# A two-layer decoder trunk on one core: operations recorded and ordered by a list scheduler inside the kernel, fixed tile homes, and another head

## The chip, the core and the metric

The kernel runs on one core of a Trainium2 chip. Such a core has a matrix engine (TensorE, PE in the profile; its weight loads are the row PEld), three engines for elementwise work (VectorE or DVE, ScalarE or ACT, GpSimd or POOL), and SyncE (SP), whose queue issues nearly all DMAs here. Every engine runs its own list of instructions strictly in the order in which the program holds it, and waits on semaphores for the others. The metric is the device time of one execution in microseconds, the median over runs.

## The reference, cut to what matters

Everything is float32, one batch, 256 positions, width 1024, two layers.

```python
def even_layer(x, ...):                       # layer 0
    h = rms_norm(x, norm_g)
    (nq, nkc, nvc, nks, nvs, nkw, nvw, ng, nz, mq, mk, mv, mz, eq, ez) = split(h @ w_in)
    kc, vc = nsa_compress(rot(nkc)), nsa_compress(nvc)          # blocks of 32 positions, small MLP
    a_out = nsa_attention(rot(nq), kc, vc, rot(nks), nvs, rot(nkw), nvw, sigmoid(ng + gate_b))
    b_out = moba_attention(rot(mq), rot(mk), mv)                # 8 heads, causal within 256
    m_out = memory_attention(eq, rms_norm(mem), w_mem_kv)       # 4 heads, 256 memory rows
    return x + concat(a_out*silu(nz), b_out*silu(mz), m_out*silu(ez)) @ w_out

def odd_layer(x, ...):                        # layer 1
    h = rms_norm(x, norm_g)
    rq, rk, rv, rz, eq, ez = split(h @ w_in)                    # 4 heads, 256 wide keys, 512 wide values
    r_out = head_group_norm(retention(rot(rq), rot(rk), rv))
    m_out = memory_attention(eq, mem_n, w_mem_kv)
    return x + concat(r_out*silu(rz), m_out*silu(ez)) @ w_out

def reference(x, mem, ...):
    return rms_norm(odd_layer(even_layer(x)), final_norm_g)
```

## The kernel before, in words

**Products.** A product with a weight matrix is made in units of eight rows of 128 input features, 512 output columns each. A weight chunk of 128x1024 floats (512 KB) is loaded from HBM into one of six `raw` buffers (`load`, L87). `split` (L118) makes two halves of it that the fast matmul format can hold: ACT casts it to `whi` (L122), DVE subtracts to get `wlo` (L123). `mm3` (L133) then multiplies three times: high by high, high by low, low by high. A chunk so costs one DMA, one ACT pass, one DVE pass and 12 matmuls of 512 columns on PE, or 24 of 256 columns in the products that come out transposed (`turned_unit`, L152).

**Order of the program.** First the head: the gate columns `nz` are multiplied while x itself arrives (L280 to L339), with three matmuls on a zeroed tile ahead of it (L320) so that PE has something to do. Then the layer-0 projections (`sparse_keys` with the weights `ksw`, `sparse_queries` with `nq`, `compress`, and so on), the four `sparse_pair`s, `memory_group`, the four `block_pairs`, the output projection, the same again for layer 1, and the final norm. Attention works on pairs of heads: scores into the two PSUM banks `s` (half-array matmuls, L100), a masked maximum on DVE (L451), an exponential on ACT (L453), scaling (L463, L465), three 128x128 transposes on PE into the single bank `t` (L252), a copy out of it by ACT (`pt`, L466), and then the products with the values into the single bank `o` (L100, again half-array). The bank `t` serves one of the two heads of a pair at a time: the second head's transposes wait for ACT's copy of the first.

**What sets the order.** The tile framework's own scheduler orders the instructions of each engine from a timeline of its own; only the first DMAs on SP and ACT are fixed by hand (L301). Tiles come from pools with a number of buffers for each tag (`raw` 6, `v4` 8, `s2` 8, `whi` and `wlo` 4); PSUM banks are `pj` 3, `s` 2, and `tr`, `t`, `o` one each. PE fills the waits of an attention chain with matmuls of a projection that comes later in the program.

Of the kernel before, what the change touches and what calls it, by code (L numbers as in the profile page):

```python
# [21 lines left out]
NV = 8  # L22
NS = 8
# [27 lines left out]

@with_exitstack
def trunk(
# [22 lines left out]
    V, S, G, PE = nc.vector, nc.scalar, nc.gpsimd, nc.tensor  # L76
    count = [0]

    def tl(tag, shape, bufs=1, dt=F32):
        count[0] += 1  # L80
        return sb.tile(shape, dt, tag=tag, bufs=bufs, name=f"{tag}_{count[0]}")

    def bank(tag):
        count[0] += 1
        return pp.tile([P, 512], F32, tag=tag, bufs=BANKS[tag], name=f"{tag}_{count[0]}")

    def load(t, src):  # L87
        nc.sync.dma_start(t, src)
        return t

    def after(ins, *others):

        for other in others:
            tc.add_manual_dep(ins.ins, other.ins.name,
                              mybir.DependencyInfo(mybir.DependencyClass.Sync, mybir.DependencyReason.DATA), reason="pair")

    def side_by_side(todo, *others):

        for i, (out, lhs, rhs, start, stop, *shared) in enumerate(todo):
            ins = PE.matmul(out, lhs, rhs, start=start, stop=stop, skip_group_check=bool(shared))  # L100
            if i == 0:
                after(ins, *others)
            else:
                tc.keep_in_program_order(ins)
# [13 lines left out]
    def split(raw, cols, tag=None):  # L118

        hi = tl(tag or "whi", [P, 1024], NV if tag else 4, F32R)[:, :cols]  # L120
        lo = tl(tag or "wlo", [P, 1024], NV if tag else 4, F32R)[:, :cols]
        S.copy(hi, raw)  # L122
        V.tensor_tensor(lo, raw, hi.bitcast(F32), ALU.subtract)  # L123
        return hi, lo
# [124 lines left out]
    def transposes(blocks, tag="t"):  # L249
        b = bank(tag)  # L250
        for i, a in enumerate(blocks):
            PE.transpose(b[:, i * P : (i + 1) * P], a, ident)  # L252
        return b[:, : P * len(blocks)]
# [27 lines left out]
    warm = tl("p", [P, 2, 512], 3)[:, 0]  # L281
    V.memset(warm, 0.0)
# [3 lines left out]
    xrow = [tl("v4", [P, D], NV) for _ in range(2)]  # L286
# [9 lines left out]
    xraw, wraw = [], []  # L296
    for q in range(4):
        if q % 2 == 0:
            xraw.append(tl("raw", [P, 1024], NRAW).rearrange("p (k t) -> p k t", k=4))
        wraw.append(tl("raw", [P, 1024], NRAW))  # L300
    with tc.manual_schedule(engines={mybir.EngineType.SP, mybir.EngineType.Activation}):  # L301
        nc.scalar.dma_start(gain0, vec[:, V_G0 : V_G0 + KT])
# [6 lines left out]
        for q in range(1, 4):
            load(xraw[q // 2][:, 2 * (q % 2) : 2 * (q % 2) + 2], xT[:, 2 * q : 2 * q + 2])  # L310
            load(wraw[q], w512[q // 2][:, (q % 2) * 1024 : (q % 2 + 1) * 1024])
        load(vect, vec)
        load(cpak, cst)
        load(posi, pos)
        load(posr, posrow.to_broadcast([P, T]))
        ahead = [load(tl("raw", [P, 1024], NRAW), w512[2][:, u * 1024 : (u + 1) * 1024]) for u in range(2)]
        for tok in range(2):
            load(xrow[tok], xtok[:, tok])
    wb = bank("t")
    for _ in range(3):  # L320
        PE.matmul(wb[:, :256], warm[:, 0:P], warm[:, :256], start=True, stop=True)
# [8 lines left out]
    for kt in range(KT):  # L330
        w = wraw[kt // 2][:, (kt % 2) * 512 : (kt % 2 + 1) * 512]
        gain_split(xraw[kt // 4], gain0, xh, xl, 4 * (kt // 4), (kt,))
        if kt == 0:
            for c0 in (0, 256):
                first_columns(w[:, c0 : c0 + 256], 0, c0, 256)
        elif kt == 1:
            first_columns(w, 1, 0, 512)
        else:
            turned_unit(ps_n, (xh, xl), *split(w, 512), (kt,), range(4))  # L339

    rstd0 = tl("rstd0", [P, 2])
    rq0 = tl("rq0", [P, 2])
# [16 lines left out]
    V.tensor_scalar(rq0, rstd0, 0.125, None, op0=ALU.mult)  # L359
# [53 lines left out]
    szn = tl("v4", [P, 4, T], NV)  # L413
# [112 lines left out]
    def sparse_keys():  # L526
        nonlocal kS, vsw
        ps = project(w512, W["ksw"], (xh, xl), tag="s")
        kS = tl("s2", [P, 2, T], NS)
# [512 lines left out]
```

## Time and profile before

| what | value |
|---|---|
| three runs | 433.09, 433.73, 435.09 µs (median 433.73) |
| the profiled execution, first to last instruction | 433.0 µs |
| PE busy | 420.4 µs (97%), 2444 rows |
| PE weight loads busy | 351.3 µs (81%) |
| DVE, ACT, POOL busy | 314.8, 250.9, 3.5 µs |
| read from HBM | 72.74 MB |
| mean granted PE clock | 0.994 |

The profiled execution lies 0.7 µs below the median of the three runs. A float32 matmul stands in the trace as two rows, a transpose and a matmul of the fast format as one. A matmul's end is modelled and overlaps the next one, so PE's rate is read from the distance between starts: a window's length divided by the number of matmuls in it.

### The profile page before, as it was taken

To read this page: it belongs to the slowest core of one execution; us is meant where nothing else is said; L and a number is where in the kernel's file an instruction comes from. 1 tells how busy PE (TensorE), PEld (TensorE's weight loads), DVE (VectorE), ACT (ScalarE), POOL (GpSimd) and SP (SyncE) were. 2 spreads that over 40 slices of the span, in tenths; PEclk is the share of its full clock that TensorE was granted. 3 is DMA by queue.
4 is the path that set the end of the run, shared out by engine and by line. 5 is a ranking of instruction groups with operands and counts; after the bars stand their busy time and mean duration, and the time that the engine had idled before them with its cause. 6 is when DMAs were issued, how large, how long until landed. Compare 5 with 4: busy or idle time off the path is not lost.

```text
span 433.0 us, 6745 instructions
## 1 busy us (share of the span) xinstructions
PE 420.4 (97%) x2444; PEld 351.3 (81%) x2444; DVE 314.8 (73%) x735; ACT 250.9 (58%) x464; POOL 3.5 (1%) x9
## 2 busy tenths in 40 slices
PE   6999999999999998989999999999999999999994
PEld 4988999889777875767888887888888888888883
DVE  4998877798876766746787996586798576676634
ACT  4765646667757668755565754546445454535703
POOL 0000000000000000000000000000000000000001
PEclk9899999999999999999999999999999999999999
DMA  7984955863435732323457454555463556566202
GB/s 234 391 290 136 322 213 201 273 217 120 145 100 162 275 118 79 98 75 120 147 163 219 132 186 147 159 165 183 145 204 109 191 195 212 179 192 195 67 2 97
DMA packets 31874, 74.22 MB, mean 171 GB/s; under 512 B 2913, under 2 KB 16481, under 8 KB 31841
## 3 DMA queue, kind: packets, MB, share of 16 engines
q1 hardware_dynamic: 31408, 73.40, 52.2%
q8 instruction: 19, 0.31, 0.3%
q10 hardware_dynamic: 432, 0.40, 0.3%
q14 instruction: 15, 0.11, 0.1%
HBM read 72.74 MB, written 1.05 MB: 170 GB/s over the span
## 4 chain that ended last, share of the span: by engine, by line
PE 94%; ACT 2%; DMA 2%; DVE 1%; SPq 0%; issue 0%; DVEq 0%; ACTq 0%
PE pj L135 19%; PE pj L137 19%; PE pj L136 19%; PE pj L194 9%; PE pj L195 4%; PE t L252 4%; PE s L100 4%; PE o L100 3%; DMA raw<-in_w 2%; PE s L135 1%; PE s L136 1%; PE s L137 1%; PE tr L135 1%; PE tr L137 1%; PE tr L136 1%; PE s L852 1%
## 5 line engine op out<-in xcount | busy, mean ns | idle before, releaser
L123 DVE TENSOR_TENSOR wlo<-raw,whi 128x1024 fp32r<-128x1024 f32 (+3 forms) x127 | 147.3, 1166 | 59.6 <-ACT whi L122 58.4
L122 ACT CAST whi<-raw 128x1024 fp32r<-128x1024 f32 (+3 forms) x127 | 126.9, 1003 | 95.8 <-PE pj L137 37.8
L136 PE MATMUL pj<-wlo,big 128*128 128x512 f32 (+2 forms) x264 | 99.3, 377 | 0.0
L137 PE MATMUL pj<-whi,big 128*128 128x512 f32 (+2 forms) x264 | 98.3, 375 | 0.0
L135 PE MATMUL pj<-whi,big 128*128 128x512 f32 (+2 forms) x264 | 98.0, 376 | 0.1
L137 PEld LDWEIGHTS pj<-whi,big 128*128 128x128 f32 x264 | 49.7, 188 | 8.9 <-issue 0.7
L194 PE MATMUL pj<-big,whi 128*128 128x512 f32 x160 | 56.8, 398 | 0.0
L135 PEld LDWEIGHTS pj<-whi,big 128*128 128x128 f32 x264 | 49.6, 188 | 8.7 <-DVE v L796 0.6
L136 PEld LDWEIGHTS pj<-wlo,big 128*128 128x128 f32 x264 | 49.7, 188 | 8.3 <-issue 0.3
L195 PE MATMUL pj<-big,wlo 128*128 128x256 f32 x160 | 44.7, 282 | 0.0
L135 PE MATMUL pj<-big,whi 128*128 128x256 f32 x120 | 35.0, 295 | 1.5 <-ACT whi L122 1.5
L194 PEld LDWEIGHTS pj<-big,whi 128*128 128x128 f32 x160 | 29.9, 188 | 7.2 <-DVE wlo L123 0.3
L136 PE MATMUL pj<-big,whi 128*128 128x256 f32 x120 | 34.7, 291 | 0.0
L137 PE MATMUL pj<-big,wlo 128*128 128x256 f32 x120 | 34.0, 293 | 0.0
L195 PEld LDWEIGHTS pj<-big,wlo 128*128 128x128 f32 x160 | 30.2, 189 | 0.8 <-issue 0.4
L135 PEld LDWEIGHTS pj<-big,whi 128*128 128x128 f32 x120 | 23.4, 196 | 2.8 <-ACT whi L122 1.7
L136 PEld LDWEIGHTS pj<-big,whi 128*128 128x128 f32 x120 | 23.5, 196 | 0.2
L137 PEld LDWEIGHTS pj<-big,wlo 128*128 128x128 f32 x120 | 23.2, 197 | 0.2 <-DVE wlo L123 0.2
L453 ACT ACTIVATE p<-p,mx 128x128 f32<-128x128 f32 (+1 forms) x48 | 21.4, 447 | 2.7 <-DVE mx L451 2.5
L252 PE MATMUL t<-cst,p 128*128 128x128 f32 x104 | 17.6, 281 | 1.8 <-ACT pt L466 1.8
L252 PEld LDWEIGHTS t<-cst,p 128*128 128x128 f32 x104 | 11.9, 140 | 7.3 <-ACT pt L466 3.0
L135 PE MATMUL pj<-whi,y 128*128 128x512 f32 x42 | 16.9, 407 | 0.0
(303 smaller groups left out, 626.3 us busy)
## 6 DMA issues: line engine op xcount, KB each, us to landing
raw<-in_w SPq DMA_DIRECT2D x91, 512.0 KB, 4.2
raw<-in_wout SPq DMA_DIRECT2D x28, 512.0 KB, 4.4
v<-in_xtok SPq DMA_DIRECT2D x4, 512.0 KB, 7.1
raw<-in_w SPq DMA_DIRECT2D x4, 280.0 KB, 3.8
v<-in_w SPq DMA_DIRECT2D x2, 512.0 KB, 6.6
raw<-in_memT SPq DMA_DIRECT2D x2, 512.0 KB, 4.9
raw<-in_memtok SPq DMA_DIRECT2D x2, 512.0 KB, 4.6
v<-in_grow SPq DMA_DIRECT2D x2, 512.0 KB, 7.0
```

What stands on the lines that cost most here:

```text
L100: ins = PE.matmul(out, lhs, rhs, start=start, stop=stop, skip_group_check=bool(shared))
L122: S.copy(hi, raw)
L123: V.tensor_tensor(lo, raw, hi.bitcast(F32), ALU.subtract)
L135: PE.matmul(ps, lh, rh, start=start, stop=False, skip_group_check=shared)
L136: PE.matmul(ps, lh, rl, start=False, stop=False, skip_group_check=shared)
L137: PE.matmul(ps, ll, rh, start=False, stop=stop, skip_group_check=shared)
L194: PE.matmul(ps[ct], wh[:, c], both[:, :, kt], start=kt == 0, stop=False, skip_group_check=True)
L195: PE.matmul(ps[ct][:, T:], wl[:, c], both[:, 0, kt], start=False, stop=kt == KT - 1, skip_group_check=True)
L252: PE.transpose(b[:, i * P : (i + 1) * P], a, ident)
L453: S.activation(p[:, hh, a], p[:, hh, a], AF.Exp, bias=mx[:, hh, tok : tok + 1], scale=-1.0, accum_out=sm[:, hh, tok : tok + 1])
L852: PE.matmul(s[:, 0:T], k[:, d, 0:P], q[:, d], start=d == 0, stop=d == 1)
```

## The change

**Recording.** `nc.vector`, `nc.scalar`, `nc.gpsimd`, `nc.tensor` and `nc.sync` are replaced by lanes of a `Plan`. A call on a lane is not issued; it is kept as an `Op` with the operations that it must follow (found from the elements that it reads and writes, a PSUM bank counting as one piece) and a price in ns. At the end of the program `plan.play()` arranges all operations and issues them engine by engine under `tc.manual_schedule()`, so the framework orders nothing any more. All engines are covered, SP's DMAs stay in the order in which they were recorded.

**Ordering.** `once` walks through time: of the engine whose next operation can start first it takes that operation. On PE an operation that has been ready for over 250 ns goes by kind (transposes, half-array matmuls and fast matmuls are kept together for a while) and then by its place in the program; on the other engines the one whose consumer on PE is due first goes first. Twelve rounds are made, each with due times from the last.

**Homes.** A tile is no longer a pool's next buffer: `home` gives each tag numbered slots, the large tags `v4` and `s2` by an explicit number at every use.

**Head.** The keys' weights `ksw` are loaded and multiplied beside `nz`, row of features by row of features, before x is complete; `ksw` is no longer a stage of its own. The order of the first DMAs is another one, the gains are issued on SP and both quarters of the first weight chunk on ACT. x and the weights have other tiles. The warm-up is nine matmuls of 128 columns on a tile that POOL zeroes. Six small DVE operations that build the rotary tables become three, and the final norm's gain is loaded after the last weights.

```diff
+class Plan:
+    def add(self, lane, method, args, kw):
+        op = self.group            # several PE calls may be one operation: plan.together()
...
+                if other is not op and (wrote or writing) and q0 < p1 and p0 < q1 and om & m:
+                    op.left.add(other)
...
+    def turn(self, mode, kind):
+        if mode == kind:
+            return 0
+        return 95 * (mode > 1 or kind > 1) + (105 if mode > 1 else 6) * (kind == 0)
+    def arrange(self):
...
+            if op.strict or op.lane == "SP":
+                if op.lane in last:
+                    last[op.lane].next.append((op, False))
...
+    def once(self):
...
+        while len(done) < len(ops):
+            best = None
+            for l in self.LANES:
+                now = free[l]
+                pick = None
+                for op in ready[l]:
+                    s = op.at
+                    key = self.order(op, l, now, s, mode)
+                    if pick is None or key < pick[0]:
+                        pick = (key, op, max(now, s))
+                if pick and (best is None or pick[2] < best[2]):
+                    best = pick
...
+    def order(self, op, l, now, s, mode):
+        early = max(s, now)
+        if l == "PE":
+            if s + SLACK > now:
+                return (3, s, op.rank)
+            if mode > 1:
+                return (2 - (op.kind > 0) - (op.kind > 1), 0, op.rank)
+            if mode == 1:
+                return (0 if op.kind else 1, 0, op.rank)
+            return ((0 if s + HOLD < now else 2) if op.kind else 1, 0, op.rank)
+        wait = 150
+        return (0 if s <= now + wait else 1, 0 if s <= now + wait else s, op.due)
+    def play(self):
+        for op in self.arrange():
+            for method, args, kw in op.calls:
+                getattr(self.engines[op.lane], method)(*args, **kw)
...
-    V, S, G, PE = nc.vector, nc.scalar, nc.gpsimd, nc.tensor
+    V, S, G, PE, SY = (plan.lane(x) for x in ("DVE", "ACT", "POOL", "PE", "SP"))
...
+    def columns(q):
+        load(xraw[q // 2][:, 2 * (q % 2) : 2 * (q % 2) + 2], xT[:, 2 * q : 2 * q + 2])
+        pairs.append([tl("raw", [P, 1024], NRAW) for c in (0, 2)])
+        step = 512 if q == 1 else 1024
+        for j in range(0, 1024, step):
+            for t, c in zip(pairs[-1], (0, 2)):
+                load(t[:, j : j + step], w512[c + q // 2][:, (q % 2) * 1024 + j : (q % 2) * 1024 + j + step])
+    with plan.fixed():
+        S.dma_start(first[0][:, 0:256], n0[:, 0:256])
+        load(gain0, vec[:, V_G0 : V_G0 + KT])
         load(xraw[0][:, 0:1], xT[:, 0:1])
+        S.dma_start(first[0][:, 256:512], n0[:, 256:512])
+        load(first[0][:, 512:1024], k0[:, 0:512])
         load(xraw[0][:, 1:2], xT[:, 1:2])
+        load(first[1][:, 0:512], n0[:, 512:1024])
+        load(first[1][:, 512:1024], k0[:, 512:1024])
...
-    for _ in range(3):
-        PE.matmul(wb[:, :256], warm[:, 0:P], warm[:, :256], start=True, stop=True)
+    for _ in range(9):
+        PE.matmul(wb[:, :P], warm, warm, start=True, stop=True)
...
+    def first_rows(wh, wl, kts):
+        for j, kt in enumerate(kts):
+            for tok in range(2):
+                ts = slice(tok * P, (tok + 1) * P)
+                cs = slice(j * 512, (j + 1) * 512)
+                mm3(ps_k[tok], xh[:, kt, ts], xl[:, kt, ts], wh[:, cs], wl[:, cs], kt == 0, kt == KT - 1)
...
-        ps = project(w512, W["ksw"], (xh, xl), tag="s")
+        ps = ps_k
...
-    szn = tl("v4", [P, 4, T], NV)
+    szn = tl("v4", [P, 4, T], at=4)
...
-        nq = heads(project(w512, W["nq"], (xh, xl)), "q")
+        nq = heads(project(w512, W["nq"], (xh, xl)), "q", 5)
...
-    gf = load(tl("v4", [P, D], NV), grow[1:2].to_broadcast([P, D]))
     acc = out_project(ys, True)
+    gf = load(tl("v4", [P, D], at=2), grow[1:2].to_broadcast([P, D]))
...
+    with tc.manual_schedule():
+        plan.play()
```

Three places in the order of PE. In the names, `whi` and `wlo` are the halves of a weight chunk, `big` the halves of x, `pj`, `s`, `t`, `tr`, `o` PSUM banks (with a `b` ahead of them in the changed kernel), `p` a softmax, `pt` its transpose.

The head of the program, PE before: the zeroed tile, then the gate columns alone, feature row 0 and 1.

```order
L321 MATMUL t_109<-p_62 128x256 x3
L327 MATMUL pj_75<-big_70,whi_115 128x256 x4
L327 MATMUL pj_76<-big_70,whi_125 128x256 x4
L327 MATMUL pj_75<-big_70,wlo_116 128x256 x2
L327 MATMUL pj_76<-big_70,wlo_126 128x256 x2
L327 MATMUL pj_75<-big_70,whi_137 128x256 x2
L327 MATMUL pj_76<-big_70,whi_137 128x256 x2
```

The same place now:

```order
L323 MATMUL bt_25_85<-p_2_62 128x128 x9
L323 MATMUL bpj_13_73<-big_9_69,whi_26_86 128x256 x4
L323 MATMUL bpj_13_73<-big_9_69,wlo_27_87 128x256 x2
L323 MATMUL bpj_14_74<-big_9_69,whi_28_88 128x256 x4
L323 MATMUL bpj_14_74<-big_9_69,wlo_29_89 128x256 x2
L323 MATMUL bs_15_75<-whi_30_90,big_9_69 128x512
L323 MATMUL bs_15_75<-wlo_31_91,big_9_69 128x512
L323 MATMUL bs_15_75<-whi_30_90,big_9_69 128x512
L323 MATMUL bs_16_76<-whi_30_90,big_9_69 128x512
L323 MATMUL bs_16_76<-wlo_31_91,big_9_69 128x512
L323 MATMUL bs_16_76<-whi_30_90,big_9_69 128x512
L323 MATMUL bpj_13_73<-big_9_69,whi_32_92 128x256 x2
```

Between the 12 gate matmuls of one feature row and those of the next now stand six of the keys, on the same row of x.

The second head-pair of `block_pairs`, PE before: values of the pair ahead, the transposes of its first and of its second head, then the output projection.

```order
L100 MATMUL o_1855<-pt_1873,v_334_1777 64x256 x2
L100 MATMUL o_1855<-pt_1873,v_334_1777 64x128 x2
L252 MATMUL t_1920<-cst_65,p_1905 128x128 x3
L252 MATMUL t_1928<-cst_65,p_1905 128x128 x3
L135 MATMUL pj_2096<-whi_2210,y_1854 128x512
```

The same place now:

```order
L323 MATMUL bo_62_122<-pt_12_72,v_3_18_78 64x256 x2
L323 MATMUL bo_62_122<-pt_12_72,v_3_18_78 64x128 x2
L323 MATMUL bt_25_85<-cst_4_64,p_74_134 128x128 x3
L323 MATMUL bpj_13_73<-big_73_133,whi_28_88 128x256
L323 MATMUL btr_39_99<-whi_26_86,y_10_70 128x512
L323 MATMUL bpj_13_73<-big_73_133,wlo_29_89 128x256
L323 MATMUL bpj_13_73<-big_73_133,whi_28_88 128x256 x2
L323 MATMUL bpj_13_73<-big_73_133,wlo_29_89 128x256
L323 MATMUL bpj_13_73<-big_73_133,whi_30_90 128x256
L323 MATMUL bt_25_85<-cst_4_64,p_74_134 128x128 x3
```

Between the two heads' transposes into the bank `t`, where nothing stood, there are now seven matmuls of layer 1's memory keys and of the output projection.

A sparse pair, PE before: transposes of one head, the scores of a later pair, then a projection.

```order
L135 MATMUL pj_1681<-whi_1702,big_70 128x512
L252 MATMUL t_1165<-cst_65,p_1140 128x128 x3
L100 MATMUL s_1270<-s_73_401,v_94_495 128x128
L100 MATMUL s_1271<-s_73_401,v_94_495 128x128
L100 MATMUL s_1270<-s_73_401,v_94_495 128x256
L100 MATMUL s_1271<-s_73_401,v_94_495 128x256
L136 MATMUL pj_1681<-wlo_1703,big_70 128x512
```

A sparse pair now:

```order
L323 MATMUL bo_62_122<-pt_12_72,s_1_52_112 64x128 x2
L323 MATMUL bt_25_85<-cst_4_64,p_2_62 128x128 x3
L323 MATMUL bs_15_75<-s_0_51_111,v_5_57_117 128x128
L323 MATMUL bs_16_76<-s_0_51_111,v_5_57_117 128x128
L323 MATMUL bs_15_75<-s_0_51_111,v_5_57_117 128x256
L323 MATMUL bs_16_76<-s_0_51_111,v_5_57_117 128x256
L323 MATMUL bo_62_122<-s_4_72_132,vcr_66_126 128x256
L323 MATMUL bt_25_85<-cst_4_64,p_2_62 128x128 x3
L323 MATMUL bpj_56_116<-whi_30_90,big_9_69 128x512
```

Here steps of three attention chains follow each other with no projection between them; in the order of the whole program the eight sparse score groups and all that follows from them now lie within less PE work than before.

More of the change, by code (lines that the diff above doesn't have):

```diff
@@ L21 @@
 EPS = 1e-6
-NV = 8
-NS = 8
 NRAW = 6
@@ L295, in trunk @@
     ps_n = [bank("pj") for _ in range(2)]
[L296 to L302, printed above, removed]
+    ps_k = [bank("s") for _ in range(2)]
+    xraw = [tl("v4", [P, D], at=2 + i).rearrange("p (k t) -> p k t", k=4) for i in range(2)]
@@ new lines, in trunk @@
+    first = [tl("raw", [P, 1024], NRAW) for _ in range(2)]
+    n0, k0 = w512[0], w512[2]
+    pairs = []
+    def columns(q):
[5 more added lines that the diff above has]
+                load(t[:, j : j + step], w512[c + q // 2][:, (q % 2) * 1024 + j : (q % 2) * 1024 + j + step])
@@ L308, in trunk @@
         S.activation(seed, seed, AF.Sin)
[L309 to L318, printed above, removed]
+        for q in range(1, 3):
+            columns(q)
@@ L328, in first_columns @@
                           start=kt == 0 and ct % 2 == 0 and a is wh and x is xh, stop=False, skip_group_check=True)
[L330 to L339, printed above, removed]
+    def first_rows(wh, wl, kts):
[4 more added lines that the diff above has]
+                mm3(ps_k[tok], xh[:, kt, ts], xl[:, kt, ts], wh[:, cs], wl[:, cs], kt == 0, kt == KT - 1)
+    with plan.fixed():
+        for kt in range(2):
+            gain_split(xraw[0], gain0, xh, xl, 0, (kt,))
+            if kt == 0:
+                for c0 in (0, 256):
+                    first_columns(first[0][:, c0 : c0 + 256], 0, c0, 256)
+            else:
+                first_columns(first[1][:, 0:512], 1, 0, 512)
+            first_rows(*split(first[kt][:, 512:1024], 512), (kt,))
+        for tok in range(2):
+            load(xrow[tok], xtok[:, tok])
+        columns(3)
+        load(vect, vec)
+        load(cpak, cst)
+        load(posi, pos)
+        load(posr, posrow.to_broadcast([P, T]))
+        for q in range(1, 4):
+            kts = (2 * q, 2 * q + 1)
+            gain_split(xraw[q // 2], gain0, xh, xl, 4 * (q // 2), kts)
+            n = 1 if q == 1 else 2
+            for i in range(0, 2, n):
+                cs = slice(i * 512, (i + n) * 512)
+                turned_unit(ps_n, (xh, xl), *split(pairs[q - 1][0][:, cs], n * 512), kts[i : i + n], range(4))
+                first_rows(*split(pairs[q - 1][1][:, cs], n * 512), kts[i : i + n])
+            if q == 1:
+                ahead = [load(tl("raw", [P, 1024], NRAW), w512[4][:, u * 1024 : (u + 1) * 1024]) for u in range(2)]
     rstd0 = tl("rstd0", [P, 2])
-    rq0 = tl("rq0", [P, 2])
     rb0 = tl("rb", [P, T], 2)
@@ L545, in compress @@
         ps = project(w280, 0, (xh, xl), 280)
-        w1t = [load(tl("v4", [P, 16, 64], NV), w1[i]) for i in range(2)]
-        w2t = tl("yf", [P, T], 2)[:, :P]
+        w1t = [load(tl("v4", [P, 16, 64], at=6 + i), w1[i]) for i in range(2)]
+        w2t = tl("w2", [P, P])
         for i in range(2):
@@ L764, in out_project @@
                 late = last and i >= total - 2
-                wh, wl = split(raw, 1024, "v4" if last and i == total - 1 else None)
+                wh, wl = split(raw, 1024, ((3, 1), (5, 0))[u] if last and i == total - 1 else None)
                 if late:
@@ L850, in ret_head @@
         s = bank("s")
-        for d in range(2):
-            PE.matmul(s[:, 0:T], k[:, d, 0:P], q[:, d], start=d == 0, stop=d == 1)
-        for d in range(2):
-            PE.matmul(s[:, T : T + P], k[:, d, P:T], q[:, d, P:T], start=d == 0, stop=d == 1)
+        with plan.together():
+            for d in range(2):
+                PE.matmul(s[:, 0:T], k[:, d, 0:P], q[:, d], start=d == 0, stop=d == 1)
+            for d in range(2):
+                PE.matmul(s[:, T : T + P], k[:, d, P:T], q[:, d, P:T], start=d == 0, stop=d == 1)
         sd = tl("p", [P, 2, 512], 3)[:, 0, :384]
```

332 lines of the change are left out of this document (270 added, 62 removed).

## The prediction, as it was put on record

> **What bounds the kernel now.** I read the page's busy times first, then the shares of the chain of waits.
>
> ```profile
> span 433.0 us, 6745 instructions
> PE 420.4 (97%) x2444; PEld 351.3 (81%) x2444; DVE 314.8 (73%) x735; ACT 250.9 (58%) x464; POOL 3.5 (1%) x9
> ...
> PE 94%; ACT 2%; DMA 2%; DVE 1%; SPq 0%; issue 0%; DVEq 0%; ACTq 0%
> ```
>
> PE is busy in 420.4 of 433.0 us and 94% of the chain is PE. An order of instructions can win only the 12.6 us in which PE is idle, and what PE does at less than its rate. Where those lie is told by windows of the span, cut at the borders of the stages:
>
> ```profile
> core 0: us, PE busy (x) PEld busy (x) DVE busy (x) ACT busy (x) POOL busy (x), PEclk, DMA share, GB/s
> 0.00:4.52 4.52, 2.93 (x6) 1.85 (x6) 1.34 (x5) 1.49 (x2) 0.57 (x6) 1.00 0.52 137
> 4.52:7.93 3.41, 2.41 (x18) 2.21 (x19) 1.90 (x4) 1.74 (x4) 0.00 (x0) 1.00 0.85 213
> 7.93:11.34 3.41, 1.93 (x15) 1.53 (x14) 1.85 (x4) 2.53 (x6) 0.00 (x0) 1.00 1.03 410
> 11.34:14.76 3.42, 3.42 (x18) 3.42 (x18) 3.42 (x8) 2.89 (x6) 0.00 (x0) 0.50 1.04 368
> 14.76:20.87 6.11, 6.11 (x52) 6.11 (x52) 5.33 (x13) 3.94 (x6) 0.00 (x0) 1.00 1.03 406
> 20.87:31.77 10.90, 10.90 (x50) 9.02 (x49) 10.21 (x35) 7.70 (x11) 0.00 (x0) 1.00 0.84 306
> 31.77:63.00 31.23, 31.23 (x216) 29.14 (x215) 25.36 (x46) 17.04 (x24) 0.31 (x1) 1.00 0.67 229
> 63.00:160.00 97.00, 97.00 (x696) 81.18 (x694) 74.39 (x215) 65.49 (x154) 0.53 (x1) 1.00 0.55 179
> 160.00:202.50 42.50, 40.03 (x241) 28.12 (x240) 26.96 (x83) 27.90 (x75) 0.00 (x0) 1.00 0.29 88
> 202.50:426.70 224.20, 224.20 (x1148) 188.65 (x1147) 162.64 (x325) 118.52 (x176) 2.04 (x1) 1.00 0.50 158
> 426.70:433.01 6.31, 0.23 (x3) 0.03 (x1) 1.40 (x5) 1.61 (x5) 0.00 (x0) 0.86 0.29 107
> ```
>
> PE has no idle time from 14.76 to 160.00 and from 202.50 to 426.70. All that can be won lies in the head (before 14.76), in 160.00 to 202.50 (2.47 us idle) and in the tail (6.1 us after the last matmul). The rows also give rates: 52 matmuls of 256 columns in 6.11 us, **0.1175 us** each; 48 of 512 columns in 10.90 us (the other two of the 50 rows are the ends of the stage ahead), **0.227 us** each. What ended PE's waits:
>
> ```profile
> PE t L252 <- ACT pt L466: 1.8, 3, 0.6
> PE pj L135 <- ACT whi L122: 1.5, 1, 1.5
> PE t L321 <- DVE root L902: 1.5, 1, 1.5
> PE pj L327 <- ACT whi L122: 1.1, 2, 0.8
> PE o L100 <- ACT pt L466: 0.6, 1, 0.6
> ```
>
> 2.6 us are waits of the head for ACT's cast of a weight chunk, 2.4 us waits for the copy `pt` out of the bank `t` or what follows it. The 1.5 us at L321 lie ahead of the warm-up.
>
> **The change part by part.** Every product stays: the order of PE holds 2250 matmuls and transposes instead of 2244, and the six are warm-up. I set the profiled execution's own 433.0 us as the base.
>
> *A, the start.* PE's first product, and what ACT did for it:
>
> ```profile
> 5.17 1.22 PE L327 MATMUL pj<-big,whi 128*128 128x256 f32 x8 [0.79 <-ACT whi L122]
> 7.21 1.21 PE L327 MATMUL pj<-big,whi 128*128 128x256 f32 x8 [0.35 <-ACT whi L122]
> 10.39 0.39 PE L135 MATMUL pj<-big,whi 128*128 128x256 f32 x1 [1.48 <-ACT whi L122]
> ...
> 4.71 0.71 ACT L122 CAST whi<-raw 128x256 fp32r<-128x256 f32 x2 [1.55 <-DMA raw<-in_w]
> 8.30 0.91 ACT L275 ACTIVATE big<-raw,gain 128x256 fp32r<-128x256 f32 x2 [1.14 <-DMA raw<-in_xT]
> 9.72 1.14 ACT L122 CAST whi<-raw 128x512 fp32r<-128x512 f32 x2 [0.51 <-DMA raw<-in_w]
> ```
>
> The cast at 4.71 waited 1.55 us for a weight DMA that ACT issued behind the gain vector's. Now the weights go first on ACT and the gain goes first on SP. The saved issue is some 0.3 us; if the bytes rather than the issue set the landing it is nothing, if x and gain are ready with it, 0.45. I take **−0.3** (−0.45 to 0).
>
> *B, the rest of the head.* From 5.17 to 31.77, the start of the next projection, 26.60 us pass for 96 matmuls of 256 columns and 48 of 512: 96 × 0.1175 + 48 × 0.227 = 22.18. So 4.42 are lost: 0.35 and 1.48 in waits, about 1.4 because the window from 11.34 to 14.76 ran at half clock (18 matmuls there, 2.1 us at the full rate, took 3.42), and some 1.2 in smaller gaps. Now each row of x feeds 12 × 0.1175 + 6 × 0.227 = 2.77 us of matmuls instead of 1.41. What PE can have by when is set by bytes. Before, feature row 2's weights ended 1.57 MB of DMAs and landed at 9.7 us:
>
> ```profile
> 3.06 6.63 DMA raw<-in_w
> 9.72 0.63 ACT whi L122
> 10.39 0.39 PE pj L135
> ```
>
> In the new order of the DMAs the gate weights of feature row 1 end at 1.05 MB (x rows 0 and 1, the first gate chunk, the first keys' chunk, this one). Before, 1.05 MB was the end of x's rows 2 and 3, on which ACT's `big` waited until 8.30 us. From there I add cast to first matmul, 10.39 − 9.72 = 0.67: PE can begin feature row 1 at about 8.95. It has feature row 0 to do from 4.87 on: 2.77 us and small gaps of 0.2 end it at 7.85, so a wait of **1.1 us** stays. Later rows need 0.65 MB each (0.13 of x, 0.26 of gates, 0.26 of keys) every 2.77 us, 237 GB/s, and the rows 7.93 to 20.87 moved 368 to 410 GB/s: no further wait. Lost after the change: 1.1 plus 0.6 of gaps (half of those before, because half as many rows of x border on each other in time) = 1.7. So B = 1.7 − 4.42 = **−2.7**. Best: only the 0.6 stay, −3.8. Worst: the wait is 1.5 longer, since the bytes of the two streams now compete, and the half clock comes again, lost 5.1, +0.7.
>
> *C, the middle.* The 2.47 us of 160.00 to 202.50 are the second heads' transposes:
>
> ```profile
> 184.21 0.55 PE L252 MATMUL t<-cst,p 128*128 128x128 f32 x3
> 184.79 0.48 ACT L466 COPY pt<-t 128x384 f32<-128x384 f32 x1 [0.23 <-PE t L252]
> 185.33 0.55 PE L252 MATMUL t<-cst,p 128*128 128x128 f32 x3 [0.57 <-ACT pt L466]
> ```
>
> Start to start 1.12 us, for three transposes of 0.109 each. The order now puts at least 1.03 us of projection between all neighbouring uses of `t`, so these waits go: −2.47. It costs a matmul taken from later, where nothing waits. Against it stands what the scheduler does elsewhere. The four sparse pairs' eight score groups lay between 82.40 and 161.10:
>
> ```profile
> 82.40:161.10 78.70, 78.70 (x507) 64.06 (x507) 61.51 (x186) 53.82 (x132) 0.00 (x0) 1.00 0.52 166
> ```
>
> Counted by the rates above, they now lie within 48.6 us of PE work. ACT's share of that, from its own groups:
>
> ```profile
> L122 ACT CAST whi<-raw 128x1024 fp32r<-128x1024 f32 (+3 forms) x127 | 126.9, 1003 | 95.8 <-PE pj L137 37.8
> ...
> L453 ACT ACTIVATE p<-p,mx 128x128 f32<-128x128 f32 (+1 forms) x48 | 21.4, 447 | 2.7 <-DVE mx L451 2.5
> L466 ACT COPY pt<-t 128x384 f32<-128x384 f32 x24 | 11.5, 477 | 8.4 <-PE t L252 8.3
> L453 ACT ACTIVATION_READ_ACCUMULATOR p<-p,mx 128x1 f32 x48 | 9.1, 189 | 0.0
> L463 ACT ACTIVATE p<-p,sm 128x256 f32<-128x256 f32 (+1 forms) x12 | 5.6, 470 | 3.9 <-DVE sm L460 3.9
> ```
>
> 9 casts of 1.003, 32 exponentials of 0.447 with 32 accumulator reads of 0.189, 16 copies of 0.477 and 8 scalings of 0.470 are 40.8 us; with 9 smaller operations that lie there too about 45 to 50 of 48.6. Rows of one engine overlap a little (two casts of 0.63 in 1.14 above), so the real load is some nine tenths, against 68% before. An in-order queue that full answers late at times, and PE, which follows a fixed order, then stands. The nearest rows are the waits of 160.00 to 202.50, about 0.6 us each; in the tightest place, where `o`, `t`, `s`, `o`, `t` follow each other with no projection, I expect one or two: **+1.0**. Bounds: none, or one of 1 us in each of the eight groups, +8 (the transposes above took 1.12 to answer). C = −2.47 + 1.0 = **−1.4** (−2.5 to +5.5).
>
> *D, the tail.* Half a row of the output is normed after the last matmul:
>
> ```profile
> 425.55 0.69 DVE L917 TENSOR_TENSOR v<-tr,v 128x512 f32<-128x512 f32 x1
> 428.36 0.16 DVE L927 RECIPROCAL ss<-ss 128x1 f32<-128x1 f32 x1 [0.90 <-ACT ss L926]
> ```
>
> The bank `pj` of the second token block now ends 14 matmuls (1.65 us) ahead of the end, where before it ended 24 (2.8 us) ahead, and one DVE product of 0.69 stands ahead of the last reciprocal. Covered by the wait for ACT (0.90) it costs nothing, uncovered 0.7. The reciprocal waits on the later of the two, so I take **+0.25**.
>
> *E, the kinds of matmul.* PE goes from one kind (fast, transposed, half-array) to another 191 times instead of 171, but has 27 half-array visits instead of 31. Sparse score rows and transposes already lie in windows with no idle time, so only spacing could tell. Twelve more round trips to transposes at the 0.008 us by which 0.1175 and 0.109 differ are 0.1; the four visits less are met by four more changes inside the visits that stay. I take **0** (−1.5 to +1, some 0.3 us a visit either way). The six DVE operations that became three, and the POOL zeroing, have DVE at 73% and POOL at 1% as cover; without it they would be worth under 0.5 us at the start of the rotary tables.
>
> Sum: −0.3 − 2.7 − 1.4 + 0.25 + 0 = **−4.15** of 433.0, a span of 428.9. The median of the three runs lies 0.7 above the profiled execution; I carry that over: **429.6 us**.
>
> **The rivals.** Two runs of this kernel can be told apart from no change above about 0.5%, so at 431.6 and 435.9.
>
> *The half clock comes again.* In 7.93 to 11.34 PE was busy for 1.93 of 3.41 us (56%), and the next window had 0.50 of the clock; in 4.52 to 7.93 it was busy for 2.41 (71%) and the clock stayed. The wait of 1.1 with small gaps would leave 2.1 to 2.3 of such a window, 62 to 67%, between the two. Price as before, 3.42 − 2.1, about 1.4: 429.6 + 1.4 = **431.0**. [...] Chance 0.20.
>
> *New waits in the denser sparse stage eat the gain.* For it speaks ACT at nine tenths, against it that the order interleaves eight chains, so one late answer has others behind it. At four to eight waits of 0.6 to 1 us more than I took, +2.4 to +6: 432 to 435.6, say **433**. Chance 0.16.
>
> *ACT becomes the bound of the sparse stage: slower.* Its work of 45 to 50 us within 48.6 stands as a queue, every exponential waits behind a cast of 1.0 us for a later chunk, and each of the eight groups is late by about the 1.12 us above, a microsecond net, +8 to what I took: **437.6**. It is slower than before from 6.3 us of new waits on. Against it: ACT's casts for later weights were ahead of PE in 63.00 to 160.00, with 37.8 us of its idle time spent on waiting for PE. Chance 0.12.
>
> *Better than forecast.* No wait of `t`, none in the sparse stage, lost 0.6 in the head: −0.45 − 3.8 − 2.5 + 0 = −6.75, **427**. For it: the scheduler knows all prices. Against it: bytes before 9 us. Chance 0.06.
>
> That the change doesn't do what it says is no case of its own: the order of PE shows the keys among the gates and projection between the transposes.
>
> **How the numbers follow.** Forecast 0.46, the others 0.20, 0.16, 0.12 and 0.06. The forecast's own range is 427 to 431.5. For the whole range I leave out most of the slower rival and half of the best: **426.5 to 435.0**. Faster by over 0.5% are the forecast, the best case and two thirds of the half clock: 0.65. Within 0.5% the third rival and the rest of the second: 0.23. Slower 0.12.
>
> **What would show it.** In the changed profile: the first product at about 4.9 instead of 5.17; one PE wait of about 1.1 between 7.8 and 9; PEclk 1.00 in 8 to 16 us; the next projection's first matmul at 28.8 to 29 instead of 31.77; no wait of transposes for `pt` at the `block_pairs`; PE idle of 1 us at most in the sparse stage; 6.3 us from last matmul to end. I am wrong if PE's idle time in the sparse stage is above 3 us, if the head's 1.1 is 2 or more, or if the spacing of like matmuls changes.

## The result, and the profile after

The changed kernel takes 431.04 us (median of 6 runs, 430.88 to 431.61); the kernel before took 433.62 us beside it (432.99 to 435.09). The ratio is 0.9938, with a 95% interval of 0.9921 to 0.9955: 0.6% faster. The forecast was 429.6 with a range of 426.5 to 435.0.

The page of the changed kernel, its span, its busy times and the shares of its chain. All operations come from one recording helper, so L323 stands for every line:

```profile
span 429.2 us, 6752 instructions
PE 420.8 (98%) x2456; PEld 353.1 (82%) x2456; DVE 321.4 (75%) x727; ACT 250.1 (58%) x464; POOL 3.6 (1%) x10
...
PE 91%; DMA 4%; ACT 1%; DVE 1%; issue 1%; SPq 0%; DVEq 0%; ACTq 0%
```

The span fell from 433.0 to 429.2, while PE's busy time stayed (420.4, now 420.8): what went is waiting. In windows cut at the borders of its own stages (time, then busy time and rows of each engine, PEclk, DMA share, GB/s):

```profile
4.85:9.03 4.18, 3.96 (x20) 3.21 (x20) 2.64 (x6) 1.75 (x3) 0.00 (x0) 1.00 0.91 271
9.03:33.00 23.97, 23.81 (x147) 21.28 (x146) 19.56 (x43) 17.08 (x25) 0.00 (x0) 1.00 0.97 353
33.00:160.00 127.00, 125.88 (x918) 105.09 (x918) 105.25 (x307) 89.25 (x214) 0.84 (x2) 1.00 0.51 172
160.00:202.50 42.50, 42.50 (x252) 35.18 (x251) 26.88 (x47) 24.42 (x49) 0.00 (x0) 1.00 0.45 144
202.50:423.29 220.79, 220.79 (x1112) 184.47 (x1110) 164.28 (x317) 113.52 (x166) 2.04 (x1) 1.00 0.50 159
423.29:429.20 5.91, 0.00 (x0) 0.00 (x0) 2.20 (x8) 1.75 (x6) 0.00 (x0) 0.72 0.42 159
```

160.00 to 202.50, where 2.47 us of PE's time were idle, has none now. But 33.00 to 160.00, which had none before, has 1.12, of which 0.96 lie between 119 and 128 us. PE's waits name them:

```profile
PE bt L323 <- POOL kcbd L323: 1.0, 1, 1.0
PE bpj L323 <- ACT whi L323: 0.6, 1, 0.6
PE bpj L323 <- DVE s L323: 0.3, 1, 0.3
PE bs L323 <- DVE wlo L323: 0.2, 1, 0.2
```

The first is the time ahead of the warm-up. No wait of transposes for the copy `pt` is left. The 0.6 for ACT's `whi` and the 0.3 for `s` are the new ones, at 120 and 126 us.

### The profile page after: what moved, and what is told of

Its sections match the earlier page's. It is cut to its first block, busy times and chain, and to the rows that moved or that the text cites. A ratio compares the mean times of both kernels' runs of the same rounds, so it can differ in the third digit from the quotient of the medians.

```text
span 429.2 us, 6752 instructions
## 1 busy us (share of the span) xinstructions
PE 420.8 (98%) x2456; PEld 353.1 (82%) x2456; DVE 321.4 (75%) x727; ACT 250.1 (58%) x464; POOL 3.6 (1%) x10
## 4 chain that ended last, share of the span: by engine, by line
PE 91%; DMA 4%; ACT 1%; DVE 1%; issue 1%; SPq 0%; DVEq 0%; ACTq 0%
PE bpj L323 69%; PE bs L323 9%; PE btr L323 5%; PE bo L323 4%; PE bt L323 4%; DMA raw<-in_w 2%; DMA v<-in_xT 2%; ACT whi L323 1%; DVE v L323 0%; DVE wlo L323 0%; DVE p L323 0%; ACT yf L323 0%; DVE s L323 0%; ACT big L323 0%; DVE rot_a L323 0%
## 5 line engine op out<-in xcount | busy, mean ns | idle before, releaser
L323 ACT CAST whi<-raw 128x1024 fp32r<-128x1024 f32 (+3 forms) x127 | 127.3, 1003 | 110.2 <-PE bpj L323 51.4
L323 DVE TENSOR_TENSOR wlo<-raw,whi 128x1024 fp32r<-128x1024 f32 (+3 forms) x127 | 146.8, 1165 | 57.9 <-ACT whi L323 57.3
L323 PE MATMUL bpj<-whi,big 128*128 128x512 f32 (+2 forms) x528 | 156.0, 377 | 1.0 <-ACT whi L323 0.6
L323 PEld LDWEIGHTS bpj<-whi,big 128*128 128x128 f32 x528 | 95.9, 188 | 19.1 <-issue 1.4
L323 PE MATMUL bpj<-big,whi 128*128 128x256 f32 (+1 forms) x416 | 108.5, 335 | 0.0
L323 PE MATMUL bpj<-wlo,big 128*128 128x512 f32 (+2 forms) x264 | 90.4, 376 | 0.0
L323 PEld LDWEIGHTS bpj<-big,whi 128*128 128x128 f32 x416 | 68.4, 191 | 3.2 <-issue 1.2
L323 PE MATMUL bpj<-big,wlo 128*128 128x256 f32 x288 | 67.4, 285 | 0.2 <-DVE wlo L323 0.2
L323 PEld LDWEIGHTS bpj<-big,wlo 128*128 128x128 f32 x288 | 52.9, 189 | 7.5 <-issue 0.7
L323 PEld LDWEIGHTS bpj<-wlo,big 128*128 128x128 f32 x264 | 49.2, 188 | 8.5 <-issue 0.3
L323 PE MATMUL bpj<-whi,y 128*128 128x512 f32 x84 | 29.0, 395 | 0.0
L323 ACT COPY pt<-bt 128x384 f32<-128x384 f32 (+1 forms) x32 | 16.2, 505 | 10.1 <-PE bt L323 9.8
L323 ACT ACTIVATE p<-p,mx 128x128 f32<-128x128 f32 (+1 forms) x48 | 21.4, 447 | 0.7 <-DVE mx L323 0.7
L323 PEld LDWEIGHTS bpj<-whi,y 128*128 128x128 f32 x84 | 15.8, 188 | 3.7 <-DVE s L323 0.2
L323 PE MATMUL bt<-cst,p 128*128 128x128 f32 x104 | 17.1, 277 | 0.0
L323 ACT ACTIVATE v<-bpj,rstd 128x512 f32<-128x512 f32 (+1 forms) x18 | 12.3, 686 | 7.6 <-PE bpj L323 7.5
L323 PE MATMUL bpj<-wlo,y 128*128 128x512 f32 x42 | 16.2, 394 | 0.0
L323 DVE TENSOR_SCALAR p<-p,sm 128x256 f32<-128x256 f32 (+1 forms) x48 | 14.4, 324 | 1.1
L323 PEld LDWEIGHTS bt<-cst,p 128*128 128x128 f32 x104 | 12.1, 140 | 3.7 <-issue 1.5
L323 DVE CUSTOM_DVE_ANT_0 p<-bs,cst 128x128 f32<-128x128 f32 (+1 forms) x48 | 14.4, 354 | 0.8 <-PE bs L323 0.7
L323 DVE TENSOR_TENSOR v<-bpj,v 128x512 f32<-128x512 f32 x6 | 4.1, 689 | 10.2 <-PE bpj L323 10.2
L323 PE MATMUL bs<-whi,big 128*128 128x512 f32 x32 | 11.1, 396 | 0.0
```

The lines of the kernel that those rows point to most:

```text
L323: getattr(self.engines[op.lane], method)(*args, **kw)
```

## The experiments

All times below are medians; the ratio is to the kernel before on the same chip, with its 95% interval. oldhead, newhead, warm1 and rush shared one chip (before: 434.49 us); homes, fill, the change and rush_again shared another (before: 434.40 us).

| kernel | head | homes | order by | us | ratio to before |
|---|---|---|---|---|---|
| homes | before's | fixed | framework | 440.95 | 1.0156 (1.0136 to 1.0177) |
| newhead | new | fixed | framework | 438.35 | 1.0097 (1.0079 to 1.0115) |
| oldhead | before's | fixed | list scheduler | 431.85 | 0.9942 (0.9924 to 0.9960) |
| fill | before's, wait filled | fixed | list scheduler | 431.65 | 0.9941 (0.9923 to 0.9959) |
| the change | new | fixed | list scheduler | 430.99 | 0.9926 (0.9907 to 0.9944) |
| warm1 | new, one warm-up | fixed | list scheduler | 430.91 | 0.9924 (0.9910 to 0.9937) |
| rush | new | fixed | list scheduler, mended | 430.35 | 0.9909 (0.9896 to 0.9922) |
| rush_again | new | fixed | list scheduler, mended | 430.23 | 0.9912 (0.9894 to 0.9930) |

**The old head under the list scheduler.**

```diff
-    with plan.fixed():                       # new DMA order, gates and keys row by row
-        S.dma_start(first[0][:, 0:256], n0[:, 0:256])
...
+    with plan.fixed():                       # before's DMA order, gates alone
+        S.dma_start(gain0, vec[:, V_G0 : V_G0 + KT])
...
-        ps = ps_k
+        ps = project(w512, W["ksw"], (xh, xl), tag="s")
```

> The changed kernel with the head of before (gate columns alone, the keys as a stage of their own, the DMAs and the warm-up as before); recording, list scheduler and fixed homes stay. Theory 1 (the terms add up: head -3.0, order -1.4 + 0.25 in the prediction): only the order's part is left, about -1 us against before, 432.3 to 433.0, with a wait of about 1.5 us before the third feature row as before, and no wait of transposes for the copy out of bank t. Rival 2 (the order carries the gain and the new head gives nothing that lasts): 431.0, as the changed kernel. Rival 3 (the order loses and the head pays for it): 434 or more.

Measured: 431.85, with an interval of some 0.8 us either way. In time it lies between theory 1's band and rival 2's 431.0, but before is slower on this chip, and both were meant against before: it is 2.6 us under before, where rival 2 had 2.6 and theory 1 about 1. So rival 2's size holds. The profiled execution is the longest of the six, 433.41 us, and its waits of PE are all ahead of or in the head:

```profile
PE bpj L323 <- ACT whi L323: 2.0, 2, 1.2
PE bt L323 <- DVE root L323: 1.5, 1, 1.5
PE bpj L323 <- DVE wlo L323: 0.2, 1, 0.2
```

In the middle there is no wait of 0.1 us or more: neither the transposes nor the sparse stage. Its six times fall in two groups. Three are 430.94 to 431.44 us with a mean granted clock of 0.996, three are 432.26 to 433.41 with 0.992 or 0.993. The windows of the profiled one show what the second group has:

```profile
5.00:8.50 3.50, 3.33 (x15) 3.33 (x16) 1.90 (x4) 1.46 (x4) 0.00 (x0) 1.00 0.82 218
8.50:12.00 3.50, 2.03 (x14) 1.62 (x12) 1.31 (x3) 1.99 (x5) 0.00 (x0) 1.00 1.04 413
12.00:15.50 3.50, 3.50 (x18) 3.50 (x19) 3.50 (x8) 3.39 (x8) 0.00 (x0) 0.55 1.03 360
```

PE is busy for 2.03 of 3.5 us, and then follows a stretch with a clock of 0.55 in which 18 matmuls start where 3.5 / 0.1175 = 30 would fit. The mean clock of a run does not hold this alone: in before's trace the granted clock is also at 0.50 from 431.18 us on, where PE has no matmul left, and that is in the mean too. So a mean of 0.996 by itself does not show a head without half clock.

**The new head under the framework's order.**

```diff
-    V, S, G, PE, SY = (plan.lane(x) for x in ("DVE", "ACT", "POOL", "PE", "SP"))
+    V, S, G, PE, SY = nc.vector, nc.scalar, nc.gpsimd, nc.tensor, nc.sync
...
-    with tc.manual_schedule():
-        plan.play()
```

> The changed kernel without recording and list scheduler: the same head and the same homes, but the framework orders the instructions as in the kernel before. Theory 1: only the head's part is left, -2 to -3 us against before, 430.6 to 431.6, with the waits of the transposes for bank t (some 2.4 us) still there. Rival 2 (the order carries the gain): 433 to 434. Rival 4 (fixed homes bind the framework, which would rotate buffers): slower than before, new waits in the middle, 435 or more.

Measured: 438.35, slower than before by 1.0%: rival 4. Its first product starts at 5.83 us, later than before's 5.17, after one wait of 0.6 us, but from there to 31 us its head loses only 1.0 us by the two rates of the prediction (0.1175 and 0.227 us a matmul), where before lost 4.4. So the head saves time, and the waits of the middle eat it; they are there, and more of them than before:

```profile
PE bt L542 <- ACT pt L781: 2.3, 4, 0.6
PE bpj L425 <- DVE rot_b L555: 1.3, 2, 0.8
...
PE bo L390 <- ACT pt L781: 0.7, 1, 0.7
```

**The fixed homes without the scheduler and the new head.** The edit of newhead, made on the kernel with the old head. It keeps the rest of the change too: x in other tiles, the three joined table operations and the final norm's gain loaded late.

> The old head, the fixed homes and the three joined table operations, ordered by the framework: neither the new head nor the list scheduler of the change. Theory H (fixed homes bind the framework, so the new head under the framework was slow for their sake): 1.006 to 1.012 of before, with as many waits in the middle as the new head under the framework had. Rival K (the keys in the head are what the framework can't use: it loses the filler that the keys' stage was): 0.998 to 1.003 of before.

Measured: 440.95, 1.6% slower than before and above the band that theory H gave; rival K is out. So the fixed homes, with those smaller edits and ordered by the framework, cost 6.6 us, and the new head takes 1.0097 / 1.0156 = 0.9942 of that, 2.6 us, close to the 3.0 that the prediction's terms A and B had together. The list scheduler under the old head is worth 0.9942 / 1.0156 = 0.979, some 9 us, of which 6.6 only repair what the homes cost. The profile shows part of that price:

```profile
PE bt L542 <- ACT pt L750: 2.5, 4, 0.7
PE bpj L425 <- ACT whi L412: 2.4, 1, 2.4
```

Since the first product PE's idle time is 6.7 us against 4.3 before. The stretch from first product to last matmul is 5.1 us longer, the tail 0.8. So some 2.7 of the 5.9 lie in PE's own spacing. Which of the edits makes them is not settled, nor how much of the 6.6 us is the homes' own.

**The waits at 120 and 126 us.** In the changed kernel ACT's cast of a weight chunk, for which PE waits, itself waited for a weight DMA:

```profile
118.34 1.05 ACT L323 CAST whi<-raw 128x1024 fp32r<-128x1024 f32 x1 [1.30 <-DMA raw<-in_w]
```

The DMA is not late for want of bandwidth. From 97 to 108 us it moves 23 GB/s, and then, from 119 us on, 384, more than the 159 with which PE had no idle time from 202.50 to 423.29:

```profile
97.00:108.00 11.00, 11.00 (x87) 9.01 (x85) 10.22 (x39) 10.24 (x30) 0.00 (x0) 1.00 0.09 23
108.00:119.00 11.00, 11.00 (x101) 9.72 (x99) 9.19 (x31) 7.72 (x20) 0.00 (x0) 1.00 0.41 136
119.00:128.00 9.00, 8.04 (x52) 6.71 (x52) 5.99 (x7) 4.48 (x6) 0.00 (x0) 1.00 1.01 384
```

DVE is busy for 10.22 of the 11 us. Among what stands in its queue are the last products of the memory rows, which read two of the six weight buffers, filled since about 75 us. ACT makes the other half of each product first, and those of the second buffer it makes only from 102.64 to 106.43. SP issues its next loads right behind DVE's last product of each buffer, at 106.00 and at 113.86:

```profile
80.01 1.27 DVE L323 SCALAR_TENSOR_TENSOR big<-raw,vec,big 128x256 fp32r<-128x256 f32 x3
105.50 0.47 DVE L323 SCALAR_TENSOR_TENSOR big<-raw,vec,big 128x256 fp32r<-128x256 f32 x1
110.44 0.48 DVE L323 SCALAR_TENSOR_TENSOR big<-raw,vec,big 128x256 fp32r<-128x256 f32 x1
111.37 0.87 DVE L323 SCALAR_TENSOR_TENSOR big<-raw,vec,big 128x256 fp32r<-128x256 f32 x2
113.31 0.48 DVE L323 SCALAR_TENSOR_TENSOR big<-raw,vec,big 128x256 fp32r<-128x256 f32 x1
...
102.64 0.89 ACT L323 ACTIVATE big<-raw,vec 128x256 fp32r<-128x256 f32 x2
105.92 0.51 ACT L323 ACTIVATE big<-raw,vec 128x256 fp32r<-128x256 f32 x1
...
106.00 0.33 SPq L323 DMA_DIRECT2D raw<-in_w  x1
113.86 0.33 SPq L323 DMA_DIRECT2D raw<-in_w  x1
```

The scheduler places them by their reader on PE, which is far off. That they also give back a buffer in which SP's next load is to land is a shorter deadline, and SP's loads stand in a fixed order behind it. The experiment makes them due sooner:

```diff
+            op.due = due - op.rush
-            op.due = due
...
-            gain_split(mraw.rearrange("p (k t) -> p k t", k=4), vect[:, V_GM : V_GM + 8], mh, ml, 4 * q,
-                       range(4 * q, 4 * q + 4))
+            with plan.soon(40000):           # op.rush = 40000 ns for what is recorded here
+                gain_split(mraw.rearrange("p (k t) -> p k t", k=4), vect[:, V_GM : V_GM + 8], mh, ml, 4 * q,
+                           range(4 * q, 4 * q + 4))
```

> The changed kernel, but the eight products of the memory rows with their gains on ACT and DVE are due 40 us sooner in the list scheduler, so that they leave the weight buffers sooner. Theory (the wait of 0.6 us for ACT whi near 120 us, and the 0.3 us after it, come from two weight buffers that DVE holds until 113 us because its queue is full of attention work, so that weights are issued late): these waits go, -0.6 to -1.0 us, the DMA rate between 97 and 108 us is no longer near 6 GB/s. Rival (the engines have no room there at all): the attention's chains come late instead, 0 to +1 us.

Measured: 430.35. In the trace DVE's products run at 71.64 and 76.31, the DMA moves 121 GB/s where it moved 23, and PE has no idle time from 86 to 128 us:

```profile
71.64 1.69 DVE L331 SCALAR_TENSOR_TENSOR big<-raw,vec,big 128x256 fp32r<-128x256 f32 x4 [0.48 <-ACT big L331]
76.31 1.67 DVE L331 SCALAR_TENSOR_TENSOR big<-raw,vec,big 128x256 fp32r<-128x256 f32 x4
...
97.00:108.00 11.00, 11.00 (x85) 8.68 (x84) 10.42 (x44) 10.40 (x31) 0.00 (x0) 1.00 0.32 121
```

ACT is as full there as before (10.40 of 11 us, 10.24 before), so a full ACT was not what PE waited for. The comparison on one chip:

> The kernel with the memory rows' products due sooner, once more, beside the unaltered changed kernel on one chip. Theory (late release of two weight buffers makes the waits of 0.6 and 0.3 us): 0.5 to 1.0 us faster than the changed kernel. Rival (the difference between calls was the chip's): within 0.3 us of it.

> The changed kernel itself, unaltered, beside the next three on one chip. Expected: 0.993 to 0.995 of before, as recorded. If the old head with the list scheduler (0.994 of before) is as fast as this, the new head's 3.0 us of the prediction are not there in the median.

Measured: 430.23 (429.88 to 430.92) against 430.99 (429.81 to 431.94) of the unaltered change, 0.76 us less, inside the theory's band. The intervals of the two ratios overlap, so the trace settles the mechanism and the medians only make its size likely. On both chips this version is 0.9% faster than the kernel before and the fastest measured. The changed kernel itself came out at 0.9926 here and at 0.9938 first; the old head under the scheduler, 0.9942, is within their intervals.

**The wait of the old head, filled.**

```diff
             elif kt == 1:
                 first_columns(w, 1, 0, 512)
+                for _ in range(6):
+                    PE.matmul(wb[:, :P], warm[:, 0:P], warm[:, :P], start=True, stop=True)
```

> The old head with the list scheduler, and six matmuls on the zeroed tile (about 1.3 us at the full clock) between the second and the third feature row, where PE waited 1.25 us. Theory (three of six runs with the old head were 1.7 us slower since an idle wait there lets the clock fall to half in some executions): no run above 432 us on a chip where before takes 434.5, median 0.3 to 1.2 us under that of the old head, spread under 1 us. Rival (the spread has another cause): spread of 2 us stays, median equal or later by up to 0.3.

Measured: 431.65 (430.60 to 432.32). The clock did as the theory says: the six means are 0.996 to 0.999, none at 0.992, and the profiled execution keeps its clock where the old head's lost it:

```profile
5.00:8.50 3.50, 3.50 (x16) 3.50 (x17) 1.84 (x5) 1.74 (x4) 0.00 (x0) 1.00 0.96 213
8.50:12.00 3.50, 3.50 (x31) 3.50 (x30) 2.27 (x5) 2.40 (x5) 0.00 (x0) 1.00 1.04 416
12.00:15.50 3.50, 3.50 (x32) 3.50 (x31) 3.50 (x8) 3.04 (x7) 0.00 (x0) 1.00 1.06 386
```

The time did not: two runs lie above 432, the spread is 1.7 us where under 1 was expected, and the ratio is that of the old head. So the half clock after the wait is real (0.55 in the old head's profile) and is gone from this profile with matmuls without use in the wait (1.00), but it is not the whole spread. The first of the three rows shows a second candidate: 16 matmuls in 3.5 us, at a clock that reads 1.00.

**One warm-up matmul instead of nine.**

```diff
-    for _ in range(9):
+    for _ in range(1):
```

> The changed kernel with one warm-up matmul instead of nine; the rest of the order is the same. Theory (the clock follows PE's busy time, as 11.34 to 14.76 of before suggests): a window of some 3.4 us before or around the first product is idle, the head starts at half clock, up to 1.7 us more for 3.4 us of matmuls, of which the waits for data hide some: +0.8 to +1.7 against the changed kernel. Rival (the clock was lost in before for another reason): within 0.3 us of the changed kernel, clock 1.00 in the head.

Measured: 430.91, with the changed kernel's 430.99 on the other chip no difference that these runs can tell, as the rival said; but not for the rival's reason. The trace has the half rate that the theory expected, and for longer than it expected:

```profile
6.24 1.05 PE L323 MATMUL bpj<-big,whi 128*128 128x256 f32 x4
7.10 0.63 PE L323 MATMUL bpj<-big,wlo 128*128 128x256 f32 x2
...
9.66 0.56 PE L323 MATMUL bs<-whi,big 128*128 128x512 f32 x1
10.07 1.10 PE L323 MATMUL bpj<-big,whi 128*128 128x256 f32 x8
11.01 0.64 PE L323 MATMUL bpj<-big,wlo 128*128 128x256 f32 x4
```

Up to 9.66 four matmuls of 256 columns take 0.86 us from start to start, 0.215 each; from 10.07 eight take 0.94, 0.1175 each. The slow matmuls replace only a part of the waiting. ACT has cast the second feature row's weights at 8.79 us here, and PE starts that row at 10.07, where it starts at 9.03 with nine warm-up matmuls. By 33 us this execution is 0.6 us behind the first profile of the changed kernel and 0.2 behind a second one. It is also the longest of its five, 431.56 us, so the trace does not show what its median run lost.

## Why the prediction was right, and where it was not

**What bounds.** Right: the gain is waiting that PE lost, and PE's rows kept their rates, the first microseconds apart.

**A, the start, −0.3.** The size is right: the first product starts at 4.85 instead of 5.17, −0.32. The saved issue is not what set it. ACT's first cast starts at 3.68, 1.03 us earlier than before, but DVE's half of x now waits for x until 4.27, where it ran at 3.39 before. With one warm-up matmul PE's wait ahead of the first product, at 4.79, names this half of x (3.01 us for DVE `big`). So the start went from waiting for weights to waiting for x, and that the difference is 0.3 is in part luck.

**B, the head, −2.7.** The direction is right, the size about 0.3 too large, and two of its steps cancelled.

```profile
4.85 1.20 PE L323 MATMUL bpj<-big,whi 128*128 128x256 f32 x4
5.85 0.47 PE L323 MATMUL bpj<-big,wlo 128*128 128x256 f32 x2
...
7.02 0.50 PE L323 MATMUL bs<-whi,big 128*128 128x512 f32 x1
7.75 0.50 PE L323 MATMUL bs<-wlo,big 128*128 128x512 f32 x1 [0.22 <-DVE wlo L323]
...
9.03 1.10 PE L323 MATMUL bpj<-big,whi 128*128 128x256 f32 x8
...
6.35 0.62 ACT L323 CAST whi<-raw 128x512 fp32r<-128x512 f32 x1 [1.56 <-DMA raw<-in_w]
7.88 0.62 ACT L323 CAST whi<-raw 128x512 fp32r<-128x512 f32 x1
7.00 0.69 DVE L323 TENSOR_TENSOR wlo<-raw,whi 128x512 fp32r<-128x512 f32 x1 [1.19 <-ACT whi L323]
```

The second feature row starts at 9.03, where 8.95 had been worked out, but not for the sum's reason. Its weights were there earlier than the sum had it: their cast starts at 7.88 and ends at 8.50. PE was still busy with the first row, which takes 4.18 us instead of 2.77. Some 0.6 of the 1.41 us lost are its first six matmuls, which are 0.22 us apart on average instead of 0.1175. Most of the rest is the first chunk of the keys: its DMA lets ACT cast only at 6.35 and DVE subtract only at 7.00, so the product with `wlo` cannot start before 7.75. The prediction looked for PE's wait between the rows, at the second gate chunk, and had no price for the keys' chunk within the first row. A second trace of the changed kernel, whose matmuls are at full rate from 5.9 on, has waits of 0.45 and 0.23 us at this chunk and starts the second row at 9.17. So the 1.41 us, where the step had 1.3, agree by luck. Summed over all rows ahead of 20 us, what the spacings have above the two rates is about 2.0, where the step had 1.7: B was −2.4 in this pair of profiles. The worst case of this term was added up wrongly (1.7 + 1.5 + 1.4 is 4.6, not 5.1), which no sum used. The sign that the next projection would begin at 28.8 to 29 can't be read off: its first matmuls, from 26.47 on, now stand between those of the keys.

**C, the middle, −1.4.** The sum is right (2.47 us of idle time went, 1.12 came) and the sparse stage's part of it, +1.0, has the right size for a wrong reason. The prediction put it on ACT's full in-order queue, answering the attention late at the tightest place; it was two weight buffers that ACT and, last, DVE gave back late, which rush shows. ACT was as full as feared, and the rival in which it becomes the bound did not happen: with ACT at 93 to 95% of 97 to 108 us, PE has no idle time there with either order, the changed kernel's or rush's.

**D, the tail, +0.25.** Wrong in sign, small. From last matmul to end it is 5.91 us, where it was 6.1:

```profile
423.99 0.69 DVE L323 TENSOR_TENSOR p<-v,v 128x512 f32<-128x512 f32 x1
424.38 0.30 ACT L323 ACTIVATE ss<-ss 128x1 f32<-128x1 f32 x1
424.71 0.17 DVE L323 RECIPROCAL ss<-ss 128x1 f32<-128x1 f32 x1
```

The DVE product of 0.69 ends at 424.68, together with ACT's last step: it is covered whole, the end of the term's bounds that was priced at nothing.

**E, the kinds of matmul, 0.** Within its bounds: −0.32, −2.4, −1.35 and −0.16 make −4.2, the span fell by 3.8, so about +0.4 remains for PE's own spacing.

**The step that failed is the base.** The span came out at 429.2, where 428.9 had been worked out; the median came out 1.4 above 429.6. The prediction added 0.7 us to the span, since the median shown lay so far above the profiled execution's span. The runs show that the time of every execution is its own span plus about 1.8: 430.99 with 429.2, 433.41 with 431.6, 430.01 with 428.2. A later run of before with a span of 433.0 took 434.84. So the profiled execution before, with 433.0, was one of about 434.8, near the longest of its runs, and the median run of before had a span near 431.8. That accounts for 1.1 of the 1.4, and the 0.3 of the span for the rest. It is also why a gain of 3.8 between two profiles is 2.6 between two medians: the waits and the half clock were priced from an execution that was some 1.2 us longer than the median one. The half clock in it, priced at 1.4, would be enough to make it so; that the median run of before had none was not shown.

**The rivals.** The half clock did not come again after the first products (1.00 from 5.99 to 425.83 us), but PE started slow (six matmuls 0.22 us apart instead of 0.1175), which the prediction had not priced. Waits in the denser sparse stage exist, at the size that the forecast took, and did not eat the gain. What no case held is how the parts add up: the prediction gave two thirds of the gain to the head, and read the homes as bookkeeping. On the chip the homes cost 1.6% where the framework orders, the scheduler earns that back with 0.6% above, and the new head then adds about 0.2%, not clear of the measurement. Under the scheduler, before the mending, it wins about 1.1 us of waits in the head of the profiled executions (1.46 with the old head, 0.39 now) and loses about as much at 120 us, where the old head under the same scheduler has none. That the keys, done early, leave the sparse stage less to fill itself with is the likely reason; it was not tried by itself. On one chip the changed kernel is 0.66 us under the old head with its wait filled (430.99 and 431.65), with intervals that overlap.

## What to carry to other kernels

An operation that frees a buffer has two deadlines, its reader's and that of the load that waits for the buffer; a scheduler that knows only the first fills a queue with work that looks urgent and starves an in-order DMA queue, which the profile shows as a stretch of low GB/s with a wait behind it (here 23 GB/s from 97 to 108 us, and PE's waits of 0.6 and 0.3 us at 120 and 126). Compare a profile with the median only after adding what lies outside the span (here about 1.8 us), measured from runs that give both, and ask whether the profiled execution was a long one before its stalls are priced as certain. Parts of a change that are priced one by one need not add up: here the fixed homes, with some smaller edits, cost 6.6 us under the framework's order, and the list scheduler over them won 9.

## What the runs showed of the hardware that was not expected

The page's row of the granted clock reads 1.00 at the start of every trace here, also where the matmuls run at half rate. In the old head, filled, 16 matmuls of 256 columns start from 5.00 to 8.50 without a wait, where 30 fit at 0.1175. With one warm-up matmul the spacing is 0.215 us up to 9.66 and 0.1175 from 10.07 on; with nine it changes before 6.2 in the first profile of the changed kernel, and before 5.9 in a second one. The trace's own clock records say the same. The first of them stands at 8.77 us in the filled old head, at 10.02 with one warm-up matmul, and at 5.99 and 4.99 in the two profiles of the changed kernel; no record stands behind what the row prints ahead of it. So the moment at which PE reaches its full rate differs between executions (the first record by 1.00 us between the two profiles of the changed kernel, by 5.03 between these four), and ahead of the first record only the distance of starts tells it. In before's trace the records stand at 4.52, 11.34, 14.76 and 431.18 us, which is 6.83, 3.41 and 416.43 us apart: 2, 1 and 122 times 3.413. The clock also fell where PE had not been idle throughout: in the old head to 0.55 in 12.00 to 15.50, after a stretch in which PE was busy for 2.03 of 3.5 us, and in before to 0.50 in 11.34 to 14.76, after 1.93 of 3.41. That the slow start makes the 1.7 us by which equal runs of the filled head differ is likely by its size, and was not shown run by run.
